# A decoder layer on one core: more Strassen sets in the down projections, residual tokens kept in DRAM

## The chip, the cores and the metric

The kernel runs on one core of a Trainium2 chip. The metric is the device time of one execution in microseconds, as the median of several runs; beside it stands one profiled execution, whose trace gives the span from the first to the last instruction.

## The reference

One decoder layer over 256 tokens of width 2048, in float32: a SwiGLU half-step FFN (inner width 5632), then a mixer (windowed attention on half of the width, a convolution module on the other half, one output projection), then a second FFN. Each of the three is followed by a residual and a LayerNorm.

```python
x = layer_norm(ALPHA * x + 0.5 * swiglu_ffn(x, ffn1...), ln1_g, ln1_b)
u = x @ w_in + b_in
...
x = layer_norm(ALPHA * x + mixed, ln2_g, ln2_b)
x = layer_norm(ALPHA * x + 0.5 * swiglu_ffn(x, ffn2...), ln3_g, ln3_b)

def swiglu_ffn(x, w_gate, w_up, w_down):
    h = jax.nn.silu(x @ w_gate) * (x @ w_up)
    return h @ w_down
```

## The kernel before

**Arithmetic.** To keep float32 accuracy, each float32 matrix is split into a high part `hi` (a rounded copy, made by ScalarE) and a low part `lo = raw - hi` (made by VectorE). A product of two blocks is then three matmuls (`mm3`, lines 624 to 626): hi·hi, hi·lo, lo·hi. A product in the FFNs has a stationary block of 128 x 128 tokens or activations and 512 columns of weights.

**Weights.** They come in units of 128 x 1024 (512 KB), one DMA each, all issued from SP's queue in the order of `sources`. `Steps` holds that order: `load` keeps up to four raw units in flight (`RAW_BUFS`), `upper` makes `hi` (L153) and `lo` (L157) of one, up to seven units ahead of TensorE (`LEAD`). The order of all engines' instructions is fixed when the program is built. `Steps.pace` runs after every product: it keeps a model of VectorE's backlog and puts in splits, or work queued in `soon`, while the backlog is under 1.2 us (`AHEAD`). `st.at(n, work)` puts work in n steps later. `drain` puts in all that `soon` holds.

**Stages of an FFN.** The inner width is cut into three parts of 16, 16 and 12 blocks (`PARTS`). In each part the up projection goes by pairs of column groups (4, 4 and 3 pairs), then the down projection of that part follows, over four chunks of 512 columns. The first pair of the first part is plain: `first_groups` in FFN1, `token_group` in FFN2. `by_sums` does all other up pairs, and the down projection of parts 0 and 1, where it takes two column chunks at a time (a column pair). The last part's down projection is plain (`tokens_by`).

**Sets.** `by_sums` runs over a string of kinds. A `C` is two weight units used as they are: eight products. An `S` is a Strassen set on two weight units: seven products, for which VectorE first makes sums and differences of the weights (four 128 x 512 steps at L171, in `first`, `second` and `third`) and then splits four results instead of two. Before, every up pair and every column pair has eight places with two S (`"SCCSCCCC"` in down). An S takes one of the four raw units (`raw`) and one of two further ones (`rawx`). After the last S of a string, `shared` adds the products that several results have in common; at the end `out` adds each result's own bank. In the down projection the residual tokens `xt` stay in SBUF; `out` adds each result's bank to them (L881), and four `plus` (L885) add `shared`'s parts.

**From up to down.** After an up pair, `gates` multiplies the gate and up halves (L949), `turn` transposes (L963), writes to DRAM in four DMAs from POOL's queue (`far`, L968), reads back (`hf`, L970), and six steps later `split` makes `hh` and `hl` (L976, L977), the stationary blocks of the down projection. For an S position `block_sums` (L926) makes sums of these too.

**Residual and norms.** FFN1 loads the tokens into `xt` in two DMAs and scales them. After the mixer, FFN2's `residuals` applies the second norm to `xt` in four chunks (L548 on VectorE, 16 steps, and ScalarE), from step 12 on, ten steps apart. At the end `norm_to_rows` makes the output: token block 0 while TensorE still works on block 1, then block 1, whose sums of three of the four chunks stay in PSUM.

Of the kernel before, what the change touches and what calls it, by code (L numbers as in the profile page):

```python
# [25 lines left out]
KINDS = ("SCCSCCCC", "SCCSCCCC", None)  # L26
BLOCKS = {"S": 7, "C": 4}
UP = (
    ((2, "C"), (3, "C"), (0, "S"), (4, "C"), (1, "S"), (5, "C"), (6, "C"), (7, "C")),
    ((0, "S"), (2, "C"), (3, "C"), (1, "S"), (4, "C"), (5, "C"), (6, "C"), (7, "C")),  # L30
)
SUMMED = (0, 1)
JG = 2
# [29 lines left out]
ZB = 5  # L63

# [7 lines left out]
ENGINES = {getattr(mybir.EngineType, e) for e in ("PE", "DVE", "Activation", "Pool", "SP")}  # L72


class Steps:
# [6 lines left out]
    def __init__(self, nc, pool, sources, head, pooled, xT, x_raw, xcat):  # L82
# [5 lines left out]
        self.paced, self.soon = False, []  # L88
        self.most = len(sources)
# [22 lines left out]

    def load(self):
# [22 lines left out]
    def load_set(self, n):  # L136

        raws = [self.raw(), self.extra.tile([P, 1024], F32, tag="rawx", name=f"rawx{n}", bufs=2)]
        self.sets += 1
        self.loaded += 3  # L140
# [52 lines left out]
    def third(self, n, raws):  # L193
# [5 lines left out]
        def ended():  # L199
            three()  # L200
            self.open -= 1
# [5 lines left out]
    def split(self):  # L207
# [7 lines left out]
        elif n is None:  # L215
            nc.scalar.copy(at[:, :, 0, :], raw)
# [113 lines left out]
def hybrid_layer(  # L330
# [29 lines left out]
    def add_ffn(wu, wd):  # L360
        for (j0, j1), kinds in zip(PARTS, KINDS):
            for g in range(j0 // JG, j1 // JG, 2):
                if g == 0:
                    sources.extend(wu[g + i, q, h] for i in range(2) for q in range(4) for h in range(2))
                else:
                    for t, kind in UP[g > 2]:
                        add_set(kind, [wu[g + i, t // 2, t % 2] for i in range(2)])
            if kinds is None:
                sources.extend(wd[c, j0 // 4 + t // 2, t % 2] for c, t in down_order(j1 - j0))
                continue  # L370
            for c in range(0, NC_, 2):
                for t, kind in enumerate(kinds, j0 // 2):
                    add_set(kind, [wd[c + i, t // 2, t % 2] for i in range(2)])

    add_ffn(wu1, wd1)
# [6 lines left out]
    add_ffn(wu2, wd2)  # L382
# [4 lines left out]
    xt = act.tile([P, 2, D], F32, tag="xt", name="xt")  # L387
    st = Steps(nc, wpool, sources, head, pooled, xT, xt.rearrange("p b (k n) -> p (b k) n", n=S), xcat)
# [41 lines left out]
    def row_chunk(r, c, name):  # L430
        t = act.tile([P, 512], F32, tag="bc", name=name, bufs=BC)
        nc.sync.dma_start(t, rows[r, c * 512 : (c + 1) * 512].partition_broadcast(P))
# [8 lines left out]
    def evacuate(ps, b, c, factor, stats, stay=False, at=0):  # L441
# [5 lines left out]
        x_ = xt[:, b, c * 512 + at : c * 512 + at + width]  # L447
# [30 lines left out]
    def norm_to_features(b, stats, par, gcol, xc):  # L478
# [39 lines left out]
        for at, plan in LN_AT[b].items():  # L518
            at += behind - SKEW if b == 1 and at >= SKEW else 0
            for late, names in enumerate(plan.split("|")):  # L520
                for name in names.split():
                    work = lambda part=parts[name[0]], c=int(name[1:] or 0): part(c)
                    work() if at == 0 else st.at(at, work, late == 1)

    def residuals(par, row, more, eng, start, every):
# [12 lines left out]
        for c in range(NC_):  # L538
            at = start + 1 + c * every

            def get(c=c, at=at):
                g, be = row_chunk(row, c, f"rg{row}_{c}"), row_chunk(row + 1, c, f"rb{row}_{c}")
                bo = row_chunk(more, c, f"ro{row}_{c}") if more is not None else None
                ys = [xt[:, b, c * 512 : (c + 1) * 512] for b in range(2)]

                def on(out, a, b_, op):
                    def work():
# [9 lines left out]
                for b in range(2):  # L557
# [3 lines left out]
                    work += [on(ys[b], ys[b], g, ALU.mult), on(ys[b], ys[b], be, ALU.add)]  # L561
                for n, x_ in enumerate(work):
                    st.at(5 + n, x_, True)
# [3 lines left out]
    def norm_to_rows(b, stats, par, gb, store, kept):  # L567

        mv, r = par[:, b, 0:2], par[:, b, 2:3]
        ys = [xt[:, b, c * 512 : (c + 1) * 512] for c in range(NC_)]  # L570
# [21 lines left out]

        if b == 0:
            scaled(0)
            rsqrt(mv[:, 1:2], r, [lambda c=c: scaled(c) for c in range(1, NC_)])
# [17 lines left out]
        if b == 0:  # L613
            for c in range(NC_):
                last(c)
        else:
# [11 lines left out]
    def block(x_, k, b):  # L628

        return x_[:, k, b * P : (b + 1) * P] if x_.shape[2] == S else x_[:, 2 * k + b]  # L630
# [117 lines left out]
    def tokens_by(lhs, k0, nk, factor, stats, finish, kept=None, lag=0):  # L748
# [7 lines left out]
        order = down_order(nk)  # L756
        skew = 0 if finish is None else SKEW if kept is None else LAST
        held, sums, halves = [], {}, []
        for n, (c, t) in enumerate(order):
            if t == 0:  # L760
                sums[c] = [psB.tile([P, 512], F32, tag="acc", name="acc0")]
                if kept is not None and c in (1, 2):
                    gu = psA.tile([P, 2, 512], F32, tag="gu", name="acc1")
                    sums[c].append(gu[:, 0])
                    halves.append(gu[:, 1, :256])
                else:
                    sums[c].append(psC.tile([P, 512], F32, tag="acc", name="acc1"))
                if kept is not None and c > 0:
# [6 lines left out]
            behind = lag if n < half - 1 else 0 if n < len(order) - skew else len(order)  # L775
# [89 lines left out]
    def down_by_sums(hh, hl, kinds, factor):  # L865

        firsts = [sum(BLOCKS[k] for k in kinds[:t]) for t in range(len(kinds))]
        places = {
            "S": ("11", "22", "12", "S1", "S2", "S3", "S4"),
# [7 lines left out]
        for c in range(0, NC_, 2):  # L877
            ys = {(i, j): xt[:, 1 - i, (c + j) * 512 : (c + j + 1) * 512] for i in range(2) for j in range(2)}
# [5 lines left out]
            def plus(y, t):  # L884
                nc.vector.tensor_tensor(out=y, in0=y, in1=t, op=ALU.add)  # L885
                st.vector(0.6)

            def shared(bank, ys=ys):

                tmp = [act.tile([P, 512], F32, tag="z", name="part", bufs=ZB) for k in range(4)]  # L890
# [607 lines left out]
```

## Time and profile before

| | |
|---|---|
| median of 3 runs | 1687.32 us (1687.31 to 1688.8) |
| profiled execution, its own time | 1688.99 us |
| its span | 1687.2 us |
| granted TensorE clock | 0.998 |
| busy share | TensorE 99%, VectorE 82%, ScalarE 54%, POOL 16% |
| TensorE's waits with a known cause | 6 us in all |

The body in order of time (from the trace): FFN1's plain pair to 49 us, up part 0 to 177, down part 0 to 263, up part 1 to 432, down part 1 to 516, up part 2 to 643, plain last down part to 706; norm, mixer and norm to 980; FFN2's plain pair to 1014, up 0 to 1143, down 0 to 1230, up 1 to 1399, down 1 to 1483, up 2 to 1610, last down part to 1676, and the last norm to the end. Matmul rows overlap in the trace, so their mean duration is longer than the distance from one to the next.

### The profile page before, as it was taken

The page shows a single profiled execution, that of the slowest core. Times are in us where ns is not written, and L with a number is a line of the kernel's source. Part 1 is how long each engine was busy: PE and PEld are TensorE (multiplying, and loading weights), DVE is VectorE, ACT ScalarE, POOL GpSimd, SP SyncE. Part 2 cuts the span into 40 slices and gives each one's busy share as a digit, 9 for nine tenths or more (in the row PEclk, how much of TensorE's full clock was granted, in tenths as well). Part 3 has the DMA queues.
Part 4 walks back from the last instruction along what each step waited for, and adds up shares of the span by engine and source line. Part 5 has one row for each costly group of instructions (what it writes and reads, how often), then busy time and mean ns, then how long its engine had stood idle before and what let it go on. Part 6 is the DMA issues. An engine that isn't in the chain of part 4 may idle for free.

```text
span 1687.2 us, 21755 instructions
## 1 busy us (share of the span) xinstructions
PE 1669.7 (99%) x7689; PEld 1383.6 (82%) x7689; DVE 1386.7 (82%) x2035; ACT 912.9 (54%) x1252; POOL 268.1 (16%) x226
## 2 busy tenths in 40 slices
PE   9999999999999999999999999999999999999997
PEld 7887788888888888888888888877888888888886
DVE  7888898789888886758887778998888888988866
ACT  6556555555555554576665465555545555545541
POOL 0100000000000000178996200000000000000000
PEclk9999999999999999999999999999999999999999
DMA  8767666567666667556654555776656665666682
GB/s 295 241 211 271 219 209 218 191 223 244 214 215 211 212 213 246 171 182 194 200 181 157 198 193 196 246 236 210 219 200 215 221 237 202 222 200 224 209 279 99
DMA packets 103694, 359.47 MB, mean 213 GB/s; under 512 B 12960, under 2 KB 13088, under 8 KB 103328
## 3 DMA queue, kind: packets, MB, share of 16 engines
q1 hardware_dynamic: 96048, 334.74, 58.6%
q0 software_dynamic: 7392, 23.08, 4.5%
q8 instruction: 60, 0.98, 0.2%
q14 instruction: 50, 0.41, 0.1%
q10 hardware_dynamic: 144, 0.26, 0.0%
HBM read 344.40 MB, written 13.63 MB: 212 GB/s over the span
## 4 chain that ended last, share of the span: by engine, by line
PE 67%; DVE 19%; DMA 6%; issue 5%; ACT 3%; DVEq 0%; POOL 0%; ACTq 0%; SPq 0%; POOLq 0%
PE sum L624 13%; PE sum L625 13%; PE sum L626 13%; DVE lo L157 9%; PE acc L624 4%; PE acc L626 4%; PE acc L625 4%; DMA raw<-in_wu 3%; ACT hi L153 2%; DVE part L1002 2%; DVE sum L171 2%; PE in_c L1149 2%; PE in_a L1149 2%; PE in_q L1149 1%; DMA raw<-in_wd 1%
## 5 line engine op out<-in xcount | busy, mean ns | idle before, releaser
L157 DVE TENSOR_TENSOR lo<-raw,hi 128x1024 fp32r<-128x1024 f32 x452 | 506.6, 1153 | 121.5 <-ACT hi L153 121.0
L153 ACT CAST hi<-raw 128x1024 fp32r<-128x1024 f32 x452 | 432.9, 996 | 298.9 <-DMA raw<-in_wu 108.1
L624 PE MATMUL sum<-hi,xcat 128*128 128x512 f32 x1080 | 420.4, 389 | 1.6 <-DVE part L1002 1.6
L625 PE MATMUL sum<-lo,xcat 128*128 128x512 f32 x1080 | 420.3, 389 | 0.6 <-DVE lo L157 0.6
L626 PE MATMUL sum<-hi,xcat 128*128 128x512 f32 x1080 | 420.2, 389 | 0.0
L624 PEld LDWEIGHTS sum<-hi,xcat 128*128 128x128 f32 x1080 | 202.7, 188 | 44.7 <-DVE part L1002 2.5
L625 PEld LDWEIGHTS sum<-lo,xcat 128*128 128x128 f32 x1080 | 202.7, 188 | 42.9 <-DVE lo L157 1.0
L626 PEld LDWEIGHTS sum<-hi,xcat 128*128 128x128 f32 x1080 | 202.7, 188 | 42.2
L968 POOL DMA_DIRECT2D far<-hr x88 | 48.8, 556 | 1167.3 <-DVE hr L963 1120.9
L236 ACT CAST hi<-raw 128x1024 fp32r<-128x1024 f32 (+1 forms) x164 | 166.6, 1030 | 119.9 <-PE acc L626 71.8
L624 PE MATMUL sum<-hi,hh 128*128 128x512 f32 x496 | 194.0, 391 | 1.9 <-DVE part L1002 1.3
L239 POOL TENSOR_TENSOR lo<-raw,hi 128x1024 fp32r<-128x1024 f32 x73 | 175.6, 2423 | 117.5 <-ACT hi L236 110.6
L626 PE MATMUL sum<-hi,hl 128*128 128x512 f32 x496 | 193.1, 389 | 0.0
L625 PE MATMUL sum<-lo,hh 128*128 128x512 f32 x496 | 193.0, 389 | 0.0
L153 ACT CAST hi<-sum 128x512 fp32r<-128x512 f32 x112 | 69.5, 622 | 139.1 <-DVE sum L171 128.9
L239 DVE TENSOR_TENSOR lo<-raw,hi 128x1024 fp32r<-128x1024 f32 (+1 forms) x91 | 106.9, 1203 | 37.9 <-ACT hi L236 37.1
L1002 DVE TENSOR_TENSOR part<-sum,part 128x512 f32<-128x512 f32 x160 | 105.1, 685 | 12.7 <-PE sum L626 8.1
L624 PEld LDWEIGHTS sum<-hi,hh 128*128 128x128 f32 x496 | 93.1, 188 | 25.1 <-DVE part L1002 3.5
L626 PEld LDWEIGHTS sum<-hi,hl 128*128 128x128 f32 x496 | 93.1, 188 | 19.4
L625 PEld LDWEIGHTS sum<-lo,hh 128*128 128x128 f32 x496 | 93.1, 188 | 18.8
L1212 DVE SCALAR_TENSOR_TENSOR conv<-hc,cw_sb,conv 128x256 f32<-128x256 f32 x231 | 96.6, 482 | 1.1
L153 ACT CAST hi<-rawx 128x1024 fp32r<-128x1024 f32 x56 | 59.0, 1053 | 48.9 <-DVE rawx L171 39.3
(198 smaller groups left out, 2319.2 us busy)
## 6 DMA issues: line engine op xcount, KB each, us to landing
raw<-in_wu SPq DMA_DIRECT2D x308, 512.0 KB, 4.8
raw<-in_wd SPq DMA_DIRECT2D x160, 512.0 KB, 4.7
raw<-in_win SPq DMA_DIRECT2D x52, 512.0 KB, 4.1
rawx<-in_wu SPq DMA_DIRECT2D x40, 512.0 KB, 6.3
raw<-in_wout SPq DMA_DIRECT2D x32, 512.0 KB, 3.7
far<-hr POOLq DMA_DIRECT2D x88, 128.0 KB, 2.7
hf<-far POOLq DMA_DIRECT2D x22, 512.0 KB, 3.6
rawx<-in_wd SPq DMA_DIRECT2D x16, 512.0 KB, 6.4
```

The lines of the kernel that those rows point to most:

```text
L153: self.nc.scalar.copy(hi, x_)
L157: self.nc.vector.tensor_tensor(out=lo, in0=x_, in1=hi.bitcast(F32), op=ALU.subtract)
L171: self.nc.vector.tensor_tensor(out=out, in0=a, in1=b, op=ALU.subtract)
L236: nc.scalar.copy(hi, raw)
L239: eng.tensor_tensor(out=lo, in0=raw, in1=hi.bitcast(F32), op=ALU.subtract)
L624: nc.tensor.matmul(ps, s_hi, m_hi, start=start, stop=False)
L625: nc.tensor.matmul(ps, s_hi, m_lo, start=False, stop=False)
L626: nc.tensor.matmul(ps, s_lo, m_hi, start=False, stop=stop)
L968: nc.gpsimd.dma_start(far[:, :, t].rearrange("f r n -> r f n"), hr[32 * t : 32 * t + 32])
L1002: nc.vector.tensor_tensor(out=out, in0=ps, in1=other, op=ALU.add)
L1149: nc.tensor.matmul(ps, w[0][:, n], x1[:, k], start=k == 0, stop=False)
L1212: nc.vector.scalar_tensor_tensor(out=out, in0=x_, scalar=w, in1=acc, op0=ALU.mult, op1=ALU.add)
```

## The change

- Down parts 0 and 1 take three S of eight (`"SCCSCSCC"`). The last part takes two S of six (`"SCCSCC"`) for the first column pair, and stays plain (`tokens_by`) for the other two chunks. An S block list may hold eight blocks (`"L"`) where the same blocks are also used plainly.
- FFN2 has two plain up pairs instead of one (`plain = 4`).
- An S set gets two of four places of its own, in a tile `more` that takes the room of `xt`; `raw` and `rawx` are no longer used for it. `load` waits with the first S until that tile is free.
- The residual tokens live in two DRAM tensors (`sides`). In FFN1 the tokens are scaled by chunks and added by an accumulating DMA (`keep_tokens`). The results of the down sets are added by four DMAs from POOL's queue for each column pair (`leave`); `plus` is gone. `tokens_back` brings the tokens back in two halves in the last part, and `stats_of` takes the statistics of the first two chunks.
- FFN2's `residuals` starts at step 1, two steps apart; the adds are accumulating DMAs from POOL's queue, and the chunks are stored to DRAM.
- In the last norm, chunks 0 and 1 of token block 0 go through ScalarE and POOL (`away`). The gains and shifts are loaded from POOL's and ScalarE's queues. Of block 1, two chunks stay in PSUM instead of three.

The diff, cut to its core:

```diff
-KINDS = ("SCCSCCCC", "SCCSCCCC", None)
-BLOCKS = {"S": 7, "C": 4}
+KINDS = ("SCCSCSCC", "SCCSCSCC", "SCCSCC")
+BLOCKS = {"S": 7, "C": 4, "L": 8}
...
             if isinstance(self.sources[n], tuple):
-                if self.sets == 2:
+                if self.sets == 2 or not self.placed():
                     return
...
     def load_set(self, n):
-        raws = [self.raw(), self.extra.tile([P, 1024], F32, tag="rawx", name=f"rawx{n}", bufs=2)]
+        k = 2 * (self.begun % 2)
+        raws = [self.places[:, k], self.places[:, k + 1]]
+        self.begun += 1
         self.sets += 1
...
-    add_ffn(wu2, wd2)
+    add_ffn(wu2, wd2, 4)
...
-    def load_tokens(b):
-        nc.sync.dma_start(xt[:, b], x[b * P : (b + 1) * P, :])
-        st.at(4, lambda: nc.scalar.mul(xt[:, b], xt[:, b], ALPHA))
+    def keep_tokens():
+        for n in range(2 * NC_):
+            b, cols = n // NC_, slice(n % NC_ * 512, (n % NC_ + 1) * 512)
+            def one(b=b, cols=cols):
+                t = act.tile([P, 512], F32, tag="bc", name="some", bufs=BC)
+                nc.gpsimd.dma_start(t, x[b * P : (b + 1) * P, cols])
+                def two():
+                    nc.scalar.mul(t, t, ALPHA)
+                    nc.gpsimd.dma_start(sides[0][b, :, cols], t, accum_op=ALU.add)
+                st.at(2, two, True)
+            st.at(96 + 8 * n, one, True)
+
+    def tokens_back(side, h):
+        if h == 1:
+            xts[0] = new_tokens()
+            st.places = st.make_places = None
+        for b in range(2):
+            cols = slice(h * 1024, (h + 1) * 1024)
+            nc.gpsimd.dma_start(xts[0][:, b, cols], side[b, :, cols])
...
                 def on(out, a, b_, op):
+                    if eng is nc.vector and op is ALU.add:
+                        return lambda: nc.gpsimd.dma_start(out, b_, accum_op=ALU.add)
...
+                def store(b):
+                    nc.gpsimd.dma_start(sides[1][b, :, c * 512 : (c + 1) * 512], ys[b])
+                    stored.append((b, c))
                 for n, x_ in enumerate(work):
-                    st.at(5 + n, x_, True)
+                    st.at(5 + n if more is not None else 3 + n // 3, x_, True)
...
+        def away(c, root):
+            if not root:
+                nc.scalar.activation(ys[c], ys[c], AF.Identity, bias=minus)
+                nc.gpsimd.tensor_tensor(out=ys[c], in0=ys[c], in1=gb[c][0], op=ALU.mult)
+            else:
+                nc.scalar.mul(ys[c], ys[c], r)
+                nc.gpsimd.tensor_tensor(out=ys[c], in0=ys[c], in1=gb[c][1], op=ALU.add)
+                store(b, c, ys[c], nc.scalar)
...
-                if kept is not None and c in (1, 2):
-                    gu = psA.tile([P, 2, 512], F32, tag="gu", name="acc1")
-                    sums[c].append(gu[:, 0])
-                    halves.append(gu[:, 1, :256])
+                if kept is not None and c == 2:
+                    halves.extend(psA.tile([P, 2, 512], F32, tag="gu", name="acc1")[:, 0, :256] for _ in range(2))
+                sums[c].append(psC.tile([P, 512], F32, tag="acc", name="acc1"))
...
-                add(tmp[3], bank[5], tmp[1])
-                add(ys[1, 1], bank[5], ys[1, 1])
-                add(tmp[2], bank[7], tmp[1])
-                for n, (at, k) in enumerate((((0, 0), 0), ((0, 1), 3), ((1, 0), 2), ((1, 1), 2))):
-                    st.soon.append(lambda y=ys[at], t=tmp[k]: plus(y, t))
-            by_sums(kinds, blocks, lambda at, ps, ys=ys: add(ys[at], ps, ys[at]), shared)
+                add(tmp[2], bank[5], tmp[1])
+                add(tmp[1], bank[7], tmp[1])
+                add(tmp[3], bank[5], tmp[1])
+                if last is not None:
+                    last()
+            def leave(at, ps, c=c, tmp=tmp):
+                t = tmp[places_[at]]
+                add(t, ps, t)
+                place = side[1 - at[0], :, (c + at[1]) * 512 : (c + at[1] + 1) * 512]
+                if more:
+                    nc.gpsimd.dma_start(place, t, accum_op=ALU.add)
+                else:
+                    nc.gpsimd.dma_start(place, t)
+            by_sums(kinds, blocks, leave, shared)
...
+                side = sides[xc is not xcat]
+                down_by_sums(
+                    hh, hl, kinds, 0.5, side, part > 0 or xc is not xcat, columns, (lambda: tokens_back(side, 1)) if ends else None
+                )
+                if not ends:
                     continue
+                tokens_back(side, 0)
                 st.paced = False
-                st.at(6, lambda: prepare(pool))
+                st.at(1, lambda: prepare(pool))
...
+                for c in range(2):
+                    for b in range(2):
+                        st.at(7 + c + 2 * b, lambda b=b, c=c: stats_of(b, c))
...
-            nc.sync.dma_start(g, rows[5, c * 512 : (c + 1) * 512].partition_broadcast(P))
-            rows3.append((g, row_chunk(6, c, f"b3{c}")))
+            nc.gpsimd.dma_start(g, rows[5, c * 512 : (c + 1) * 512].partition_broadcast(P))
+            rows3.append((g, row_chunk(6, c, f"b3{c}", nc.scalar)))
...
-        x2, "2", BEHIND, lambda: residuals(par2, 3, None, nc.vector, 12,10), prepare3,
-        lambda b, s: norm_to_rows(b, s, par3, rows3, store, kept), kept,
+        x2, "2", BEHIND, lambda: residuals(par2, 3, None, nc.vector, 1, 2), prepare3,
+        lambda b, s: norm_to_rows(b, s, par3, rows3, store, kept),
+        lambda: more_places() if len(stored) == 2 * NC_ else None, kept,
```

More of the change, by code (lines that the diff above doesn't have):

```diff
@@ L72, with up_of, blocks_of @@
 ENGINES = {getattr(mybir.EngineType, e) for e in ("PE", "DVE", "Activation", "Pool", "SP")}
+def up_of(g, j0, plain):
+    return 0 if g == plain else 2 if g == j0 // JG else 1
+def blocks_of(columns):
+    return lambda kind: BLOCKS["L" if kind == "S" and columns < NC_ else kind]
 class Steps:
@@ L111, in raw, with placed @@
         return self.pool.tile([P, 1024], F32, tag="raw", name=f"raw{n}", bufs=RAW_BUFS)
+    def placed(self):
+        if self.places is None and self.make_places is not None:
+            self.places = self.make_places()
+        return self.places is not None
     def load(self):
@@ L569, in norm_to_rows @@
         mv, r = par[:, b, 0:2], par[:, b, 2:3]
[L570 removed]
+        ys = [xts[0][:, b, c * 512 : (c + 1) * 512] for c in range(NC_)]
         ins = [kept.get((b, c), [ys[c]]) for c in range(NC_)]
@@ L591, in last @@
             store(b, c, ys[c], nc.sync)
-        if b == 0:
-            scaled(0)
-            rsqrt(mv[:, 1:2], r, [lambda c=c: scaled(c) for c in range(1, NC_)])
+        minus = par[:, b, 3:4]
+        def away(c, root):
[6 more added lines that the diff above has]
+                store(b, c, ys[c], nc.scalar)
+        if b == 0:
+            nc.vector.tensor_scalar(out=minus, in0=mv[:, 0:1], scalar1=-1.0, scalar2=None, op0=ALU.mult)
+            for c in range(AWAY):
+                away(c, False)
+            scaled(AWAY)
+            rsqrt(mv[:, 1:2], r, [lambda c=c: scaled(c) for c in range(AWAY + 1, NC_)])
         else:
@@ L613, in norm_to_rows @@
         if b == 0:
-            for c in range(NC_):
+            for c in range(AWAY, NC_):
                 last(c)
+            for c in range(AWAY):
+                away(c, True)
         else:
@@ L756, in tokens_by @@
         order = down_order(nk)
+        if k0 == 0:
+            order = [x_ for x_ in order if x_[0] > 1]
         skew = 0 if finish is None else SKEW if kept is None else LAST
@@ L774, in tokens_by @@
             held.append((c, t, w))
-            behind = lag if n < half - 1 else 0 if n < len(order) - skew else len(order)
+            behind = len(order) if n >= len(order) - skew else lag if n < half - 1 else 0
             while len(held) > behind:
@@ L863, in by_sums, with down_by_sums @@
                 st.step(0)
-    def down_by_sums(hh, hl, kinds, factor):
-        firsts = [sum(BLOCKS[k] for k in kinds[:t]) for t in range(len(kinds))]
+    def down_by_sums(hh, hl, kinds, factor, side, more, columns, last):
+        firsts = [sum(map(blocks_of(columns), kinds[:t])) for t in range(len(kinds))]
         places = {
-            "S": ("11", "22", "12", "S1", "S2", "S3", "S4"),
+            "S": ("21", "11", "22", "12", "S1", "S2", "S3", "S4")[-blocks_of(columns)("S"):],
             "C": ("21", "11", "22", "12"),
@@ L875, in blocks @@
             return hh[:, n], hl[:, n]
-        for c in range(0, NC_, 2):
-            ys = {(i, j): xt[:, 1 - i, (c + j) * 512 : (c + j + 1) * 512] for i in range(2) for j in range(2)}
+        for c in range(0, columns, 2):
+            tmp, places_ = [], {(0, 0): 0, (0, 1): 2, (1, 0): 1, (1, 1): 3}
             def add(out, ps, other):
@@ L882, in add, with shared, ffn @@
                 st.vector(0.62, 0.3)
[L884 to L890, printed above, removed]
+            def shared(bank, tmp=tmp):
+                tmp.extend(act.tile([P, 512], F32, tag="z", name="part", bufs=ZB) for k in range(4))
                 nc.scalar.mul(tmp[0], bank[1], factor)
                 add(tmp[1], bank[6], tmp[0])
+                add(tmp[2], bank[5], tmp[1])
+                add(tmp[1], bank[7], tmp[1])
                 add(tmp[3], bank[5], tmp[1])
-                add(ys[1, 1], bank[5], ys[1, 1])
-                add(tmp[2], bank[7], tmp[1])
-                for n, (at, k) in enumerate((((0, 0), 0), ((0, 1), 3), ((1, 0), 2), ((1, 1), 2))):
-                    st.soon.append(lambda y=ys[at], t=tmp[k]: plus(y, t))
-            by_sums(kinds, blocks, lambda at, ps, ys=ys: add(ys[at], ps, ys[at]), shared)
-    def ffn(xc, tag, skew, begun, prepare, finish, kept=None):
+                if last is not None:
[9 more added lines that the diff above has]
+            by_sums(kinds, blocks, leave, shared)
+    def ffn(xc, tag, skew, begun, prepare, finish, places, kept=None):
         with tc.tile_pool(name=f"ffn{tag}", bufs=2) as pool:
-            st.extra, st.act = pool, act
+            st.act, st.make_places = act, places
             lhs = (xc[:, :, 0, :], xc[:, :, 1, :])
@@ L938, in ffn @@
                 ends = part == len(PARTS) - 1
-                count = 2 * n if kinds is None else sum(BLOCKS[k] for k in kinds)
+                columns = 2 if ends else NC_
+                count = sum(map(blocks_of(columns), kinds))
                 hh, hl = (pool.tile([P, count, P], F32R, tag=t, name=f"{t}{part}", bufs=1) for t in ("hh", "hl"))
```

94 lines of the change are left out of this document (57 added, 37 removed), and 1 row of the table UP.

## The prediction

> **What bounds the kernel now.** I read the page's busy line first, then the table by stage, then TensorE's own waits, and last the stretches that the change rewrites.
>
> ```profile
> span 1687.2 us, 21755 instructions
> PE 1669.7 (99%) x7689; PEld 1383.6 (82%) x7689; DVE 1386.7 (82%) x2035; ACT 912.9 (54%) x1252; POOL 268.1 (16%) x226
> L626 PE MATMUL sum<-hi,xcat 128*128 128x512 f32 x1080 | 420.2, 389 | 0.0
> ```
>
> TensorE is busy in 99% of the span, and VectorE, the next, in 82%. One matmul row lasts 389 ns, but that is no price: rows overlap. The price is the spacing, read from a stage that never stalls. Its columns are length, then busy time and count of PE, PEld, DVE, ACT, POOL, then clock, DMA share and GB/s.
>
> ```profile
> 49.10:177.10 128.00, 127.15 (x560) 104.48 (x559) 109.19 (x142) 70.27 (x89) 10.45 (x18) 1.00 0.67 230
> 177.10:263.10 86.00, 85.27 (x373) 69.41 (x373) 76.41 (x96) 45.38 (x55) 2.77 (x5) 1.00 0.64 218
> 263.10:431.80 168.70, 168.70 (x746) 139.69 (x745) 142.69 (x181) 88.61 (x111) 8.32 (x15) 1.00 0.64 216
> 431.80:516.10 84.30, 84.30 (x373) 69.81 (x372) 74.24 (x94) 44.40 (x53) 2.77 (x5) 1.00 0.65 221
> 1013.90:1143.40 129.50, 127.74 (x559) 104.40 (x558) 116.36 (x159) 74.47 (x99) 8.36 (x15) 1.00 0.64 217
> 1143.40:1229.90 86.50, 85.40 (x373) 69.44 (x373) 77.16 (x97) 44.74 (x54) 2.77 (x5) 1.00 0.64 217
> 1398.50:1483.30 84.80, 84.69 (x373) 69.57 (x373) 75.52 (x95) 44.20 (x54) 2.77 (x5) 1.00 0.65 222
> ```
>
> The third row is four up pairs: 168.70 / 746 = 0.226 us a matmul. A product (three matmuls) is 0.68 us. At that price 373 matmuls are 84.3 us, so the four down stages (rows 2, 4, 6 and 7) lose 1.7, 0, 2.2 and 0.5 us. The first up stages (rows 1 and 5: 558 matmuls of the kernel, 126.2 us) lose 1.8 and 3.3. The whole body therefore holds some 9 us of stalls; the rest is matmuls back to back. The causes:
>
> ```profile
> PE sum L624 <- DVE part L1002: 2.9, 4, 0.9
> PE acc L624 <- DVE st L455: 0.8, 1, 0.8
> PE sum L625 <- DVE lo L157: 0.8, 2, 0.6
> ```
>
> All are VectorE being late: a bank not yet emptied (L1002), a weight not yet split (L157).
>
> [...]
>
> **The change, part by part.**
>
> *Products.* A Strassen set (S) takes 7 products where a pair (C) takes 8. Per FFN the down parts 0 and 1 go from two to three S of eight, over two column pairs: 2 x 2 x 1 = 4 products fewer. The last part goes from none to two S of six, on one column pair: 2 fewer. FFN2's second up pair (groups 2 and 3) becomes plain: 2 S lost, 2 products more. In all 12 - 2 = 10 products, 30 matmuls x 0.226 = -6.8 us. By the 389 ns of a row it would be 11.7; the spacing excludes that.
>
> *What the sets cost VectorE.* Rows of down part 1 (two column pairs, 4 S and 12 C):
>
> ```profile
> L157 DVE TENSOR_TENSOR lo<-raw,hi 128x1024 fp32r<-128x1024 f32 (+1 forms) x33 | 37.0, 1154 | 7.0 <-ACT hi L153 7.0
> L157 DVE TENSOR_TENSOR lo<-sum,hi 128x512 fp32r<-128x512 f32 x8 | 5.1, 683 | 0.0
> L885 DVE TENSOR_TENSOR xt<-xt,part 128x512 f32<-128x512 f32 x8 | 5.0, 682 | 0.0
> L157 DVE TENSOR_TENSOR lo<-rawx,hi 128x1024 fp32r<-128x1024 f32 x4 | 4.9, 1217 | 0.0
> L171 DVE TENSOR_TENSOR sum<-rawx,sum 128x512 f32<-128x512 f32 x4 | 2.8, 692 | 0.1
> L171 DVE TENSOR_TENSOR raw<-raw,sum 128x512 f32<-128x512 f32 x4 | 2.7, 687 | 0.1
> L171 DVE TENSOR_TENSOR rawx<-rawx 128x512 f32<-128x512 f32 x4 | 2.7, 684 | 0.0
> L171 DVE TENSOR_TENSOR sum<-rawx,raw 128x512 f32<-128x512 f32 x4 | 2.7, 676 | 1.2 <-DMA rawx<-in_wd 1.2
> L153 ACT CAST hi<-raw 128x1024 fp32r<-128x1024 f32 (+1 forms) x33 | 31.8, 999 | 25.6 <-DMA raw<-in_wd 16.7 <-DVE raw L171 4.0 <-DMA raw<-in_wu 3.2
> ```
>
> One S: L171 (2.8 + 2.7 + 2.7 + 2.7) / 4 = 2.7, two halves 5.1 / 4 = 1.3, rawx 1.2, a full raw 1.2, a half raw 0.7: 7.1 us. One C: two full raws, 2.4. Each S adds 4.7 us of VectorE for 0.68 us of TensorE. Against that the four `plus` (L885) of a column pair go, 4 x 0.63 = 2.5: net +2.2 a column pair, +4.4 a stage. The down stages then need 80.8, 78.6, 81.6 and 79.9 us of VectorE inside 122 products x 0.68 = 83.0: 80.2 on average, 97%. I cost this at nothing, because VectorE need only keep its lead: in the last row above ScalarE waits 16.7 us for `in_wd` and VectorE in turn 7.0 for ScalarE; that is a ring of four raw places in which each S holds one, and S gets four places of its own. The cover is 83.0 - 80.2 = 2.8 us a stage and the lead at its start; without it the price is the second rival's. Bounds on the net of these stages: -4.4 (all their stalls go) to +29. I take 0, nearest to the full-pace up stage, where S sets at 85% stall nothing.
>
> *FFN2's residual.*
>
> ```profile
> L548 DVE TENSOR_TENSOR xt<-xt,rg 128x512 f32<-128x512 f32 x8 | 5.5, 683 | 0.0
> ```
>
> Its 16 VectorE steps (this row and as many adds), spread from step 12 over the first up stage, go to steps 1 to 13 over plain groups; the 8 adds become DMAs on POOL's queue. That stage loses 3.3 us now against FFN1's 1.8; I take the difference, -1.5 (0 to -3.3). Four pairs of row loads stay on SP; the fourth needs the first one's buffers, freed by an add on POOL, and holds the weights queued behind it by a step or so. The cover is the lead of up to seven split weights, a plain one lasting 4 x 0.68 = 2.7 us.
>
> *The last down part.* It needs the blocks of the last turn at index 4 of six: 7 + 8 + 8 + 7 products, 20.4 us after its start. Now they are due after eight plain weights, 21.7. How fast a turn is after a stage of sets (stages that begin at 431.8 and 1398.5):
>
> ```profile
> 438.23 1.42 DVE L949 TENSOR_TENSOR ht<-part 128x256 f32<-128x256 f32 x4
> 446.26 0.56 POOL L970 DMA_DIRECT2D hf<-far  x1 [2.72 <-DMA far<-hr]
> 452.23 1.05 ACT L153 CAST hi<-raw 128x1024 fp32r<-128x1024 f32 x1 [3.97 <-DMA raw<-in_wd]
> 453.19 1.13 ACT L976 CAST hh<-hf 128x512 fp32r<-128x512 f32 x2
> 454.46 1.28 DVE L977 TENSOR_TENSOR hl<-hf,hh 128x512 fp32r<-128x512 f32 x2
> 1406.21 1.42 DVE L949 TENSOR_TENSOR ht<-part 128x256 f32<-128x256 f32 x4
> 1414.56 0.56 POOL L970 DMA_DIRECT2D hf<-far  x1 [2.74 <-ACT hi L153]
> hf<-far POOLq DMA_DIRECT2D x22, 512.0 KB, 3.6
> ```
>
> `hf` is issued 14.5 and 16.1 us in, lands 3.6 later (18.1 and 19.7), and cast and subtraction take some 0.6 each: ready at 19.3 to 20.9. With the present order, where a cast behind a late raw goes first, the first block was ready only at 454.46 + 0.6, 23.3 us in. So TensorE waits between 0 and 2.9 us, in both FFNs; I take the middle, +1.45 x 2 = +2.9.
>
> *DMAs and POOL.* New on POOL's queue: per FFN 20 results of the down sets and 4 reloads of tokens; beside them 8 x-chunks in and 8 accumulated, 8 residual adds and 8 stores, 4 gains of the last norm. 84 issues x 0.56 (the `hf` rows) = 47 us on an engine that is 16% busy; some 21 MB more, 12 GB/s beside the 213 to 230 of the stages above.
>
> ```profile
> xt<-in_x SPq DMA_DIRECT2D x2, 1024.0 KB, 8.6
> out<-xt SPq DMA_DIRECT2D x7, 256.0 KB, 2.7
> ```
>
> No accumulating DMA is in this trace. By the nearest rows a 256 KB one lands in 2.7 us, at most in the 8.6 of a 1 MB load. The result tiles it reads are wanted again by the next `shared`, some 28 us on, so I take 0. In POOL's queue a waiting add or reload holds back the next turn's `far` and `hf`: in FFN2's plain groups, where a turn has six steps to spare, and in the last part, where only the gains stand behind it. Behind the last part's four results stand the reload (1 MB) and the statistics on VectorE seven steps (19 us) later: 8.6 + 8.6 = 17.2, still inside; the upper bound is a few us there. The added casts, about two more of L153's 1.0 us a set, meet a ScalarE at 54%: 0.
>
> *The tail.*
>
> ```profile
> 1670.59 2.74 DVE L588 SCALAR_TENSOR_TENSOR xt<-xt,par,b 128x512 f32<-128x512 f32 x4
> 1673.25 0.69 DVE L449 SCALAR_TENSOR_TENSOR acc<-acc,xt 128x512 f32<-128x512 f32 x1
> 1674.79 0.39 PE L624 MATMUL acc<-hi,hh 128*128 128x256 f32 x1 [0.78 <-DVE st L455]
> 1679.14 1.26 POOL L610 TENSOR_TENSOR xt<-xt,g 128x512 f32<-128x512 f32 x1
> 1679.57 1.40 DVE L588 SCALAR_TENSOR_TENSOR xt<-acc,par,b 128x512 f32<-128x512 f32 x2
> 929.00 2.45 DVE L239 TENSOR_TENSOR lo<-raw,hi 128x1024 fp32r<-128x1024 f32 x1 [3.06 <-ACT hi L236]
> ```
>
> Two chunks of token block 0 leave VectorE (four steps of 0.7), so the evacuation at 1673.25 comes up to 2.8 us sooner, and the halves get tiles of their own: the 0.78 us stall goes. Against it block 1's second chunk is now read from `xt` instead of a bank, beside POOL's 1.26 us step at 1679.14. The row at 929.00 is a subtraction of two SBUF tiles beside POOL work: 2.45 us where such a one takes 1.2. So a delay of up to 1.3 us is possible. ScalarE's queue now also carries this block's two stores, each waiting for POOL; behind them stands only the second chunk's scaling. I take -0.4 (-0.8 to +0.5). [...]
>
> **The sum** against the profiled span: -6.8 + 0 - 1.5 + 2.9 - 0.4 = -5.8, so 1681.4. The profiled execution took 1688.99 (1.8 more than its span); the median of three runs is 1687.32, and the same difference gives **1681.5 us**.
>
> **The rivals.**
> *All lateness goes.* The deeper raw places end the waits for `in_wd`, the last turn is in time, and the body's stalls fall from 9 to some 4: -6.8 - 5 gives 1675.5 to 1679. For it: ScalarE's 16.7 us. Against: most stalls are banks (L1002), which more raw places do not empty.
> *The gain is spent on waiting.* The last turn costs its full 2.9 twice and the denser down sets 0.5 a stage: -6.8 + 5.8 + 2 - 1.9 = -0.9, within 0.2%: 1684 to 1690.
> *TensorE has room.* The products dropped leave idle time behind: -6.8 does not arise, and what is left of the sum is within 0.2%, 1688. Against: 168.70 us without a gap. [...]
> *VectorE becomes the bound (slower).* In part 1 of FFN1 it idles 84.3 - 74.2 = 10.1 us; the same idling on top of 80.2 needs 90.3 us where products take 83.0: 7.3 us a stage, 29 in all, and 1710.5 at full price. It decides from the point where more than 2.8 + (5.8 + 3.4) / 4 = 5.1 of those 10.1 us stay. Against: VectorE enters these stages some weights ahead, and an up stage leaves 26 us to catch up.
>
> **How the numbers follow.** Forecast 0.54 (1679 to 1684), all lateness gone 0.16, gain spent 0.17, TensorE with room 0.03, VectorE the bound 0.10. 0.2% (3.4 us) is about what this measurement tells from no change; so faster 0.70, same 0.20, slower 0.10. The range 1677 to 1688 leaves out the slower rival and the far end of the first.
>
> **What would show it.** By stage: down parts at 367 matmuls in 83 to 84.5 us with VectorE near 80; the last part's set stage at 46 products, 138 matmuls, in 31.2 us plus the wait for `hl`. TensorE's waits on `lo` (L157's successor) under 2 us in all. FFN2's first up pairs without the residual's steps. If down stages last over 86 us, or TensorE waits on a reload or on POOL, I am wrong.

## The result, and the profile after

The changed kernel takes 1705.13 us (median of 4 runs, 1703.05 to 1707.55); beside it the kernel before took 1688.06 (1687.31 to 1688.89). The ratio is 1.0104, with a 95% interval of 1.0092 to 1.0116: 1.0% slower, where 1681.5 us, faster, was forecast. The profiled execution took 1707.55 us, its span 1705.7, 18.5 more than before.

The busy line and TensorE's waits (engine, tile and line waiting, what it waited for; us in all, times, longest):

```profile
span 1705.7 us, 21964 instructions
PE 1666.1 (98%) x7659; PEld 1382.4 (81%) x7659; DVE 1418.7 (83%) x2102; ACT 938.3 (55%) x1301; POOL 338.7 (20%) x314
PE sum L697 <- DVE ht L1031: 8.0, 1, 8.0
PE tp L533 <- DVE z L549: 7.2, 1, 7.2
PE sum L698 <- DVE lo L175: 2.5, 1, 2.5
```

The 30 matmuls are gone (7689 to 7659), and the busy shares look as before: 83% for VectorE says nothing of what happened. Two single waits of 8.0 and 7.2 us do. Before, no wait in the body was over 0.9 us.

The stretches of the four down stages, and of the first microseconds after each of the two long waits (columns as in the prediction):

```profile
176.16:259.10 82.94, 82.94 (x367) 68.72 (x366) 76.01 (x96) 46.20 (x57) 5.51 (x10) 1.00 0.64 220
427.76:511.90 84.14, 83.49 (x367) 68.56 (x366) 76.83 (x98) 47.42 (x61) 8.76 (x13) 1.00 0.77 238
1161.57:1244.50 82.93, 82.93 (x367) 68.69 (x366) 75.30 (x96) 46.24 (x59) 6.44 (x10) 1.00 0.69 226
1413.17:1496.10 82.93, 82.93 (x367) 68.69 (x366) 76.01 (x96) 46.26 (x57) 7.19 (x10) 1.00 0.66 218
706.90:711.40 4.50, 4.38 (x15) 3.72 (x16) 4.44 (x6) 2.38 (x6) 0.00 (x0) 0.50 0.10 16
1080.90:1085.20 4.30, 4.09 (x10) 3.27 (x11) 3.27 (x6) 1.87 (x3) 2.12 (x4) 0.52 0.55 187
```

The denser down stages run at full pace, 83.0 us for 122 products, but for one stall of 1.2 us: what the change was made for came about. In the last two rows the clock is about half; in the first case it stayed at 0.50 until 712.9, 6.0 us in all. By stage, from the first matmul of one to the first of the next, after minus before:

| part of the span | before | after | difference |
|---|---|---|---|
| FFN1 up 0 and down 0 | 214.02 | 209.92 | -4.1 |
| FFN1 up 1, down 1, up 2 | 379.4 | 379.3 | -0.1 |
| FFN1 last down part | 62.34 | 60.98 | -1.4 |
| first norm (last matmul ahead of its transposes to the first one behind them) | 14.77 | 24.87 | **+10.1** |
| FFN2 plain pairs and up 0 | 163.64 | 177.17 | **+13.5** |
| FFN2 down 0 and down 1 | 171.3 | 165.92 | -5.4 |
| FFN2 last down part | 66.34 | 66.37 | 0 |
| from the start of the last matmul to the end | 11.0 | 16.8 | **+5.8** |

Gains of 11.0 stand against losses of 29.4 in three places. Each loss is a round trip through DRAM over POOL's queue.

*FFN2's residual.* POOL's, SP's, ScalarE's and VectorE's rows in order of time (start, duration, in brackets the idle time before and what ended it), and the wait of SP's queue:

```profile
1016.64 0.92 POOL L594 DMA_DIRECT2D xt<-rb  x1 [39.14 <-DVE xt L597]
1030.15 0.57 POOL L616 DMA_DIRECT2D y<-xt  x1 [8.56 <-DMA xt<-rb]
1050.56 0.55 POOL L616 DMA_DIRECT2D y<-xt  x1 [5.92 <-DMA xt<-rb]
1067.68 0.57 POOL L616 DMA_DIRECT2D y<-xt  x1 [1.02 <-DMA xt<-rb]
1070.23 0.80 SPq L160 DMA_DIRECT2D more<-in_wu  x2
1073.68 1.04 ACT L171 CAST hi<-more 128x1024 fp32r<-128x1024 f32 x1 [9.36 <-DMA more<-in_wu]
1075.10 0.69 DVE L189 TENSOR_TENSOR sum<-more 128x512 f32<-128x512 f32 x1 [9.53 <-DMA more<-in_wu]
SPq L160 <- DMA y<-xt: 12.1, 1, 12.1
```

`y<-xt` is the store of a finished chunk to DRAM. Each store waits on POOL for the accumulating add before it (8.56, 5.92 us), and every later issue, `far` and the next add among them, stands behind it. (`far` and `hf` are the write and read of a turn.) The first set of up part 0 needs the tile `more`, which takes the room of `xt`, and its load waits on SP for the last store: 12.1 us, with all weights queued behind. ScalarE and VectorE then idle for 9.4 and 9.5 us, all of TensorE's lead is used up, and it waits 8.0 us for `ht` (L1031), a step that stands behind those splits on VectorE.

*End of FFN1.* VectorE's row of the kernel before, then POOL's and VectorE's rows of the changed kernel:

```profile
704.01 2.72 DVE L505 SCALAR_TENSOR_TENSOR z<-xt,par,rp 128x512 f32<-128x512 f32 x4
```

```profile
673.70 0.88 POOL L976 DMA_DIRECT2D y<-part  x1 [19.20 <-DVE part L956]
675.44 1.79 POOL L976 DMA_DIRECT2D y<-part  x2 [0.85 <-DVE part L956]
681.82 0.86 POOL L976 DMA_DIRECT2D y<-part  x1 [4.58 <-DVE lo L257]
690.85 1.20 POOL L472 DMA_DIRECT2D xt<-y  x2 [8.17 <-DMA y<-part]
697.15 0.70 DVE L1147 BATCH_NORM_STATS2 st<-xt 128x6 f32<-128x512 f32 x1 [2.68 <-DMA xt<-y]
706.12 2.72 DVE L549 SCALAR_TENSOR_TENSOR z<-xt,par,rp 128x512 f32<-128x512 f32 x4
```

From the first accumulating DMA of the last part (673.70) to the first statistic on the reloaded tokens (697.15) pass 23.4 us, where the prediction had 17.2 at most against a slack of 19. The norm's `z`, which the transposes need, comes at 706.12. TensorE starts its last matmul ahead of them at 699.39 and then waits 7.2 us; before, that matmul started at 704.96 and `z` at 704.01, in time.

*The tail.* The same chain at the end, with VectorE's last steps:

```profile
1657.60 0.88 POOL L976 DMA_DIRECT2D y<-part  x1 [18.91 <-DVE part L956]
1675.13 1.21 POOL L472 DMA_DIRECT2D xt<-y  x2 [7.06 <-DMA y<-part]
1678.55 1.29 DVE L1147 BATCH_NORM_STATS2 st<-xt 128x6 f32<-128x512 f32 x2 [0.47 <-DMA xt<-y]
1683.23 1.41 DVE L1147 BATCH_NORM_STATS2 st<-xt 128x6 f32<-128x256 f32 x4 [3.39 <-DMA xt<-y]
1692.04 0.69 DVE L493 SCALAR_TENSOR_TENSOR acc<-acc,xt 128x512 f32<-128x512 f32 x1
1698.12 1.73 DVE L645 SCALAR_TENSOR_TENSOR xt<-xt,par,b 128x512 f32<-128x512 f32 x1
1698.05 1.26 POOL L681 TENSOR_TENSOR xt<-xt,g 128x512 f32<-128x512 f32 x1
```

The statistics of block 0's reloaded chunks (128x512) come at 1678.55, those of block 1's (taken in halves, 128x256) at 1683.23, 25.6 us after the first result was sent off. In VectorE's order of instructions block 0's last sums (1684.55) and its norm (from 1686.36) stand behind both. So block 0's norm runs beside and after block 1's matmuls, whose last started at 1688.98; that block's sums are taken up only at 1692.04.

### The profile page after: what moved, and what is told of

Read it like the earlier page. It is cut to its first block, busy times and chain, and to the rows that moved or that the text cites. A ratio compares the mean times of both kernels' runs of the same rounds, so it can differ in the third digit from the quotient of the medians.

```text
span 1705.7 us, 21964 instructions
## 1 busy us (share of the span) xinstructions
PE 1666.1 (98%) x7659; PEld 1382.4 (81%) x7659; DVE 1418.7 (83%) x2102; ACT 938.3 (55%) x1301; POOL 338.7 (20%) x314
## 5 line engine op out<-in xcount | busy, mean ns | idle before, releaser
L175 DVE TENSOR_TENSOR lo<-raw,hi 128x1024 fp32r<-128x1024 f32 x328 | 386.1, 1220 | 71.6 <-ACT hi L171 71.0
L697 PE MATMUL sum<-hi,xcat 128*128 128x512 f32 x1026 | 399.7, 390 | 9.6 <-DVE ht L1031 8.0
L698 PE MATMUL sum<-lo,xcat 128*128 128x512 f32 x1026 | 399.5, 389 | 2.5 <-DVE lo L175 2.5
L699 PE MATMUL sum<-hi,xcat 128*128 128x512 f32 x1026 | 399.4, 389 | 0.0
L171 ACT CAST hi<-raw 128x1024 fp32r<-128x1024 f32 x328 | 331.1, 1048 | 78.3 <-DMA raw<-in_wu 26.4
L171 ACT CAST hi<-more 128x1024 fp32r<-128x1024 f32 (+1 forms) x198 | 179.8, 908 | 180.8 <-DVE more L189 147.3
L697 PEld LDWEIGHTS sum<-hi,xcat 128*128 128x128 f32 x1026 | 192.7, 188 | 50.5 <-DVE ht L1031 8.5
L697 PE MATMUL sum<-hi,hh 128*128 128x512 f32 x580 | 225.8, 389 | 0.7 <-DVE part L956 0.7
L175 DVE TENSOR_TENSOR lo<-more,hi 128x1024 fp32r<-128x1024 f32 (+1 forms) x198 | 202.1, 1042 | 28.7 <-ACT hi L171 28.6
L699 PE MATMUL sum<-hi,hl 128*128 128x512 f32 x580 | 225.6, 389 | 0.0
L698 PE MATMUL sum<-lo,hh 128*128 128x512 f32 x580 | 225.6, 389 | 0.0
L699 PEld LDWEIGHTS sum<-hi,xcat 128*128 128x128 f32 x1026 | 192.7, 188 | 40.1
```

The lines of the kernel that those rows point to most:

```text
L171: self.nc.scalar.copy(hi, x_)
L175: self.nc.vector.tensor_tensor(out=lo, in0=x_, in1=hi.bitcast(F32), op=ALU.subtract)
L697: nc.tensor.matmul(ps, s_hi, m_hi, start=start, stop=False)
L698: nc.tensor.matmul(ps, s_hi, m_lo, start=False, stop=False)
L699: nc.tensor.matmul(ps, s_lo, m_hi, start=False, stop=stop)
```

## The experiments

**The two chains, one at a time and together.** `e1_adds_on_vector` makes the residual's adds on VectorE again, `e2_last_part_local` keeps the last part's sums in SBUF, `e3_both` does both.

```diff
 # e1
-                    if eng is nc.vector and op is ALU.add:
-                        return lambda: nc.gpsimd.dma_start(out, b_, accum_op=ALU.add)
 # e2: tokens_back for both halves in `last`, and in `leave`:
+                if last is not None:
+                    y = xts[0][:, 1 - at[0], (c + at[1]) * 512 : (c + at[1] + 1) * 512]
+                    st.at(4, lambda: nc.vector.tensor_tensor(out=y, in0=y, in1=t, op=ALU.add))
+                    return
```

> The change, with the eight adds of FFN2's residual put back on VectorE; the eight stores to DRAM stay on POOL's queue. Theory A (round trips): the changed kernel lost its time where a chain of DMAs on POOL's queue ends late; here the chain add, store, add, store that held the first Strassen weights until 1070 us. Without the adds the stores are done some 15 us earlier, TensorE's waits of 8.2, 2.7 and 1.7 us in FFN2's first up pairs go, and the time falls by 11 to 15 us to 1690 to 1694. Theory B (VectorE too dense, the prediction's slower rival): eight more VectorE steps of 0.6 us, no gain, 1705 to 1710.

> The change, with the last part's results added to the tokens by four VectorE steps; both halves of the tokens are read back right after the last Strassen set, so nothing goes to DRAM and back at the end of an FFN. Theory A: TensorE's 7.4 us wait in FFN1's norm with the slow matmuls behind it (9 to 10 us) goes, and the tail shrinks from 16.7 us to some 11 with the 2 us of waits ahead of it: 15 to 18 us less, 1687 to 1690. Theory B: four more VectorE steps in each FFN, no gain, 1705 to 1710.

> Both edits together. Theory A: the two gains add up, 26 to 33 us less than the changed kernel, 1672 to 1679, under the kernel before by the 10 products (6.8 us) and some stalls of the down parts. Theory B: 1705 or more.

Measured: e1 1688.1 us, ratio to the kernel before 1.0005 (0.9995 to 1.0015); e2 1689.47, 1.0004 (0.9994 to 1.0014); e3 1674.4, 0.9921 (0.9907 to 0.9936). Against the changed kernel that is -17.0, -15.7 and -30.7: the two effects add up almost without overlap. TensorE's longest waits, first of e1, then of e2, then of e3:

```profile
PE tp L533 <- DVE z L549: 4.1, 1, 4.1
```

```profile
PE sum L697 <- DVE ht L1035: 8.3, 1, 8.3
```

```profile
PE idle L416 <- DVE ones L413: 1.2, 1, 1.2
PE sum L694 <- DVE part L953: 1.0, 2, 0.9
```

In e1 the wait for `ht` is gone and the norm's stays (4.1 us); in e2 it is the other way round, with the norm's stretch back at 14.8 us and the tail at 12.2; in e3 both are gone and the tail is 11.0, as before. So these two chains are the whole loss, and without them the change is worth 14 us.

**What in the residual's chain holds the weights.** `e4_stores_behind` leaves the accumulating DMAs but moves all eight stores behind the eight adds in POOL's queue.

```diff
-                    st.at(5 + n if more is not None else 3 + n // 3, x_, True)
+                    st.at(5 + n if more is not None else 3 + n // 3 if n < 7 else 13 - 2 * c, x_, True)
```

> The change, with the residual's eight stores issued together at step 15, behind all the accumulating adds, in place of each behind its chunk's adds. Theory A1 (the order in POOL's queue: a store that waits for an add to land holds back the next chunk's adds): the chain ends some 10 us earlier, most of the 8.2 us wait goes, 1692 to 1697. Theory A2 (the accumulating DMAs themselves are slow, whatever stands behind them): the wait stays, 1703 to 1707. Theory B: no change.

Measured: 1697.23 us, ratio 1.0054 (1.0037 to 1.0071), 7.9 less than the changed kernel. POOL's rows of e4:

```profile
1034.14 2.69 POOL L594 DMA_DIRECT2D xt<-rb  x3
1041.65 0.87 POOL L594 DMA_DIRECT2D xt<-rb  x1 [4.82 <-issue]
1050.10 1.61 POOL L616 DMA_DIRECT2D y<-xt  x3 [0.35 <-issue]
```

The last store is issued at 1051 instead of 1067.68, and the wait for `ht` falls from 8.0 to 0.8. But a wait of 3.7 on `lo` follows 18 us later (2.5 in the changed kernel), and SP's load of `more` still waits 10.0 us for the last store, against 12.1. So the order in POOL's queue is about half of e1's 17.0 us; for the other half, adds and stores done without DMAs that add, e1 is the evidence, and this run does not part it further. The first load of `more` shows the same division: it goes out 85.8 us after FFN2's first matmul in the changed kernel, 78.3 in e4 and 67.8 in e1.

**What in the last part's chain is long.** `e7_plain_writes_at_end` sends the last part's four results by plain DMAs; it leaves out their sum with what parts 0 and 1 brought, so its output isn't the layer's, and only its time is of use. `e9_larger_ring` raises the program's `dynamic_dma_scratch_size` from 1024 to 1536, and drops a small tile that nothing uses.

```diff
 # e7
-                if more:
+                if more and last is None:
                     nc.gpsimd.dma_start(place, t, accum_op=ALU.add)
 # e9
-dynamic_dma_scratch_size=1024
+dynamic_dma_scratch_size=1536
-    const.tile([P, 40], F32, name="fill")
```

> The change, with the last part's four results written to DRAM by plain DMAs instead of accumulating ones (so the last part is not added to the sums of the parts before it). Theory A (the way to DRAM and back): a plain write lands some 3 us sooner (5.1 against 8.0 us median in the changed kernel), so of the 15.7 us that the local adds brought, 3 to 8 come; 1697 to 1702. If the accumulation alone were the cause: all 15, 1688 to 1691.

> The change with 1536 in place of 1024 bytes of scratch a partition for the descriptors of POOL's DMAs (an unused 160-byte tile makes room). In the changed kernel the fourth of four accumulating DMAs is issued 0.3 us after the first has landed, some 5 us late, though its data were ready (681.82 after 681.51, 1667.20 after 1666.89). Theory A3 (the descriptors' room holds only three): the fourth follows at once, both reloads start 2 to 5 us sooner, and 3 to 9 us of the 15.7 come back: 1696 to 1702. If something else holds it, nothing changes: 1703 to 1707.

Measured: e7 1691.28 us, ratio 1.0024 (1.0012 to 1.0036), 13.8 less than the changed kernel and far below what was expected of it. e9 1700.67, ratio 1.0078 (1.0055 to 1.0102), its four runs from 1695.22 to 1706.46. POOL's rows of FFN1's last part, e7 and then e9:

```profile
671.86 0.55 POOL L978 DMA_DIRECT2D y<-part  x1 [18.19 <-DVE part L956]
673.60 1.74 POOL L978 DMA_DIRECT2D y<-part  x3 [1.18 <-DVE part L956]
683.72 1.18 POOL L472 DMA_DIRECT2D xt<-y  x2 [8.38 <-DMA y<-part]
```

```profile
671.06 0.88 POOL L976 DMA_DIRECT2D y<-part  x1 [17.87 <-DVE part L956]
672.77 2.68 POOL L976 DMA_DIRECT2D y<-part  x3 [0.82 <-DVE part L956]
687.29 1.24 POOL L472 DMA_DIRECT2D xt<-y  x2 [11.84 <-DMA y<-part]
```

With plain DMAs the reload goes out 11.9 us after the first result, and the norm's wait is 0.7 us. With accumulating ones it took 17.2 us. That in the changed kernel the fourth goes out after 4.6 us of idling (6.1 in the tail) is not the reason: with 1536 all four go out without it (`x1`, then `x3`), and the reload still follows only 16.2 us after the first (17.7 in the tail). In e1 and e4, where this part is as in the changed kernel, it follows after 17.1 and 16.9 (16.4 and 18.7 in the tail), so the larger size gains nothing that stands out. The accumulation itself makes it long: issued alike, the four accumulating DMAs of e9 left POOL idle for 11.84 us ahead of the reload, the four plain ones of e7 for 8.38. The expectation for e7 put a landing 3 us sooner at 3 to 8 us in all; it overlooked that the wait in front of TensorE and the half clock behind it (below) go too, and that the chain stands in the kernel twice. The time lies just above what its other theory, the accumulation as the only cause, gave (1688 to 1691). The gain of e9's median over the changed kernel is 4.5 us, but its runs spread over 11 us, so no size is read from it.

**What the rest is worth.** `e5_two_sets` is e3 with the old two S of eight in the down parts; `e6_norm_on_vector` is e3 with the last norm's first chunks on VectorE; `e10_both_again` and `e11_norm_on_vector_again` repeat e3 and e6 beside each other.

```diff
 # e5
-KINDS = ("SCCSCSCC", "SCCSCSCC", "SCCSCC")
+KINDS = ("SCCSCCCC", "SCCSCCCC", "SCCSCC")
 # e6, e11
-AWAY = 2
+AWAY = 0
```

> The version with both edits, with two Strassen sets of eight in down parts 0 and 1 in place of three. Theory A: the denser sets cost TensorE nothing and each set saves a product: 8 products of 0.68 us come back, 5.4 us over the version with both edits (1674.4), so 1678 to 1681. Theory B (VectorE at 97% in these stages slows them): no slower than 1674.4, perhaps faster.

> The version with both edits, with all four chunks of token block 0's last norm on VectorE (AWAY = 0). If moving two chunks off VectorE is worth what the prediction said (a wait of 0.8 us in front of the last matmuls, up to 2.8 us of VectorE time ahead of block 1's norm): 0.4 to 3 us over 1674.4. If POOL's steps beside VectorE's two-input steps cost as much as they save: 1674 to 1675.

> The version with both edits again, beside the two that follow: 1673 to 1676.

> Both edits with token block 0's last norm all on VectorE, again and on the same chip: by the trace's tail (12.9 us behind the last matmul against 11.0) 1.5 to 2.5 us over the run before; if the earlier difference was the chip's, no difference.

Measured: e5 1683.4 us (ratio 0.9973, 0.9962 to 0.9984), 9.0 above e3's median, where 4 to 7 were expected, and 7.3 above it in span: 4 x 1.37 us of matmuls, as expected, and one wait of 2.2 us. Its other three down stages run at full pace too. e10 1674.78 (0.9922, 0.991 to 0.9935), e3 again. e6 1676.37 (0.9934, 0.9918 to 0.995) and e11 1675.56 (0.993, 0.9916 to 0.9944): 2.0 and 0.8 above e3 and e10, with overlapping intervals; the tail is 12.9 us in e6's trace against 11.0 in e3's. But e5 and e12, which have the norm's edit, have tails of 12.2 and 12.1. So the edit seems worth some 1 to 2 us, and these runs can't tell it from nothing.

**Is VectorE near its limit?** `e8_three_sets_up` is e3 with a third S in 13 up pairs, `e12_third_set_some_pairs` with a third S in only the first pair of up parts 1 and 2.

```diff
-SUMMED = (0, 1)
+SUMMED = (0, 1, 2)
 # in UP, e8 in the entry of 13 pairs, e12 in another (4 pairs)
-    ((0, "S"), (2, "C"), (3, "C"), (1, "S"), (4, "C"), (5, "C"), (6, "C"), (7, "C")),
+    ((0, "S"), (3, "C"), (4, "C"), (1, "S"), (5, "C"), (2, "S"), (6, "C"), (7, "C")),
 # both: the sums of the third S's token blocks
-                            st.at(4, lambda m=m: st.soon.append(lambda: sums_of(m)))
+                            st.at(2, lambda m=m: sums_of(m), True)
```

> The version with both edits, and a third Strassen set in 13 of the up pairs (order S C C S C S C C, with token sums for a third weight position). It asks where VectorE does become the bound. An up pair then has 61 products, 41.5 us, for some 35.7 + 4.7 = 40.4 us of VectorE, 97%, as the down stages have now, but for up to six column pairs on end, with no slack stage between. If 97% is enough: 13 x 0.68 = 8.8 us less, 1664 to 1667. If VectorE's idling in these stages can't shrink that far, TensorE waits on splits and sums and the time is over 1674.

> Both edits, and a third Strassen set in only the first up pair of parts 1 and 2 (four pairs of the whole kernel, 4 x 0.68 = 2.7 us of products). Theory C (VectorE bounds only where dense pairs follow each other without slack): a dense pair after a down stage and before slack pairs costs nothing, 1671 to 1673. If a single pair of three sets is already too much for VectorE, each loses 2 us or more: 1676 to 1684.

Measured: e8 1721.32 us, ratio 1.0197 (1.0181 to 1.0213), 47 above e3. e12 1678.5, ratio 0.995 (0.9937 to 0.9962), 3.7 above e10. The stretch of FFN1's up part 1 in e8, and TensorE's longest waits in the whole of e8:

```profile
268.81:442.00 173.19, 169.61 (x736) 137.08 (x735) 154.30 (x205) 94.76 (x124) 19.39 (x31) 1.00 0.73 235
PE sum L694 <- DVE part L1084: 12.6, 27, 1.3
PE sum L695 <- DVE lo L175: 9.0, 19, 0.8
```

FFN1's up part 1 and FFN2's up part 0, first in e3 and then in e12:

```profile
258.87:427.50 168.63, 168.63 (x745) 139.64 (x744) 143.88 (x186) 92.89 (x118) 19.42 (x31) 1.00 0.76 242
1052.30:1136.90 84.60, 84.60 (x374) 69.76 (x373) 75.64 (x101) 45.43 (x60) 5.59 (x10) 1.00 0.65 221
```

```profile
259.40:427.40 168.00, 168.00 (x743) 139.11 (x742) 147.79 (x193) 93.94 (x121) 19.36 (x31) 1.00 0.76 241
1051.85:1140.46 88.61, 86.56 (x374) 70.69 (x372) 78.64 (x108) 46.61 (x62) 5.57 (x10) 0.98 0.62 215
```

In e8 TensorE waits for VectorE (27 + 19 of its short waits are these two), which is busy for 154.30 of 173.19 us, 89%. Its idling shrinks only from 24.7 us in e3 to 18.9; 14.9 of that are waits for ScalarE's casts, which in turn wait for VectorE's sums (102.6 us, and 227.1 and 157.8, in the whole of e8). So the two engines don't get to the 97% that was asked, and far more is lost than the products save. In e12 each of the four stages with one denser pair gets 0.6 to 0.7 us shorter, a product's price, as the theory that expected a gain had it. The total is nevertheless higher: 4.0 us are lost in FFN2's up part 0 and 0.9 in FFN1's, which have no denser pair. What differs in FFN2's is seven more VectorE steps (101 to 108), where the sums of the third S's token blocks are now made, at the start of the first set pair; a wait of 1.9 us on `lo` and a stretch at a lower clock (0.61 over 4.4 us) follow there. Another 1.1 us stands in the tail, without a cause that the trace names. So e12 does not say that the denser pairs cost more than they bring, only that this version of them does; the sums at another place were not tried.

**The best version** is e3, run twice: 1674.4 and 1674.78 us, 0.8% below the kernel before.

## Why the prediction was wrong

*Products, -6.8: right.* The spacing held (the last part's set stage took 31.3 us, forecast 31.2), and none of the idle time of the rival "TensorE has room" appeared: TensorE ran at full pace in the stages above.

*Denser down sets, 0: better than that.* The four stages lost their stalls but for 1.2 us, so the term was -3.2, near the good end of -4.4. The density is not what ended the stalls: in e5, with two S, three of the stages have none either. Which other part of the change did was not tested. VectorE needed 75.3 to 76.8 us of the 83.0, not 80.2. The forecast added two S to stretches that held more than their own work: VectorE splits ahead, and the four stretches had 34, 33, 34 and 34 whole weight splits before and 31, 32, 31 and 31 after. A smaller part is that rows overlap (in FFN1's down part 1, 98 rows add up to 83.8 us and cover 76.8), which adding up means counts twice.

*FFN2's residual, -1.5: the first step that failed.* "Holds the weights queued behind it by a step or so" named the right queue and the wrong wait. That wait is there, 6.4 us on SP; the one that starved TensorE is the next, 12.1 us for the last store. The stage got 13.5 us longer; undoing the adds gives back 17.0. On POOL's queue the prediction counted 84 issues at 0.56 us, and of the waits between them only those that hold back a turn: not the eight adds and eight stores, each store behind its add, one after the other. That `load` now waits for the whole tile `more`, and so for the last store, was in the diff and not in the sum. The gain that was forecast is real: in e3, with the adds on VectorE, the stage is 1.4 us shorter than before though it holds two products more.

*DMAs and POOL, 0: the second that failed, and about as large.* "17.2, still inside" took the landing of a 1 MB load as the upper bound for four accumulating DMAs of 256 KB. They took 17.2 us by themselves, and the reload 6.3 more. It cost 10.1 us in the first norm and most of 5.8 in the tail; e2 gives back 15.7. The changed kernel's accumulating DMAs of results (L976) and its plain ones from the same queue (L978), with the time of an issue and to the landing:

```profile
L976 POOL DMA_DIRECT2D y<-part x32: 853/880/1203, 471.8 to 1667.2; - x32
DMA to landing us min/median/max: 5.1/8.0/12.2
L978 POOL DMA_DIRECT2D y<-part x8: 539/542/569, 218.5 to 261.0; - x8
DMA to landing us min/median/max: 3.4/5.1/6.3
```

One lands after 8.0 us in the median and up to 12.2, so 8.6 was no upper bound, and 2.7 far too low even for a plain one here. And four of them in one chain took longer than the slowest one: 17.2 us against 12.2.

*Last turn, +2.9: 0.* No wait of TensorE on `hl` shows in either FFN.

*Tail, -0.4: about -0.8 without the reload.* In e3 the wait of 0.8 us ahead of the last matmuls is gone, as forecast, and the time behind them is 11.0 us, as before. The delay of up to 1.3 us beside POOL's step is there, 1.0 us long: L645 took 1.73 us beside L681 (0.74 the next time, reading a bank). What in the two steps holds the one back is not shown.

*The rivals.* The slower rival had the right sign with the wrong cause: VectorE was not the bound in the down stages, and e8 shows where TensorE begins to wait for it. With both chains out, e3 reaches 1674.4, just below the range of "all lateness goes" (1675.5 to 1679), and some 2 of the body's 9 us of stalls are left in it. None of the rivals was a round trip through DRAM, though the text named its two ends; the chance of 0.10 for slower stood on a mechanism that did not act.

## What to carry to other kernels

A chain of DMAs that wait for each other is priced by its longest path, issue to landing for each link, against the slack at its far end, and where the links are of a kind that the trace doesn't show, a bound from other DMAs is no bound: here 17.2 us was forecast at most and 23.4 came. In a queue where an issue that waits holds back those behind it, as on POOL here (8.56 and 5.92 us of waiting for an add), put what can go at once ahead of what has to wait: here moving eight stores, each of which waits for its add, behind the eight adds gave 7.9 us. And a change can hold a good part and a bad one: take the suspects out one at a time and together before giving up the whole.

## What the runs showed of the hardware

- The granted clock was 0.50 and 0.52 right after TensorE had waited 7.2 and 8.0 us (the last two stretches of the table of down stages), for 6.0 and about 4 us; matmuls came 0.43 us apart instead of 0.226. So each of the two waits cost about 10 us (an estimate: the wait, and half of the stretch behind it). Matmuls 0.43 us apart also followed the wait of 4.1 us in e1; none followed the one of 2.5 us in the changed kernel, where the clock was 1.00 over the next 4.4 us. In e12 matmuls 0.43 us apart came after a wait of 1.9 us, from 0.8 us behind its end on. So the length of the wait alone does not tell in these runs when the clock falls. The stretch behind that wait in e12:

```profile
1078.60:1083.00 4.40, 4.37 (x12) 3.46 (x13) 4.40 (x4) 2.44 (x3) 0.00 (x0) 0.61 0.46 142
```

- An accumulating DMA of 256 KB from POOL's queue occupied the queue for 0.88 us in the median, a plain one for 0.54, and was on its way for 8.0 against 5.1 (the rows of L976 and L978 above).

- With a `dynamic_dma_scratch_size` of 1024, a fourth accumulating DMA behind three went out after 4.6 and 6.1 us of idling; with 1536 (e9) it followed at once, and so did the fourth of four plain ones (e7) with 1024. In the chain this shows no gain: 16.2 and 17.7 us to the reload in e9, against 17.2 and 17.5 in the changed kernel.
